# Hybrid decoder trunk on one core: another bank pool for the second half of the last gate, and a fixed place for the block transposes

## The chip, the core and the metric

The kernel runs on one core of one Trainium2 chip (TRN2). The metric is the device time of one execution in microseconds (us), and the time of a kernel is the median of its runs. The engines are named as in the profile: PE is TensorE (PEld its weight loads), DVE is VectorE, ACT is ScalarE, POOL is GpSimd, SP is SyncE, which here only issues DMAs.

## The reference

One layer over 512 tokens of width 1024 in float32: a norm, one input projection shared by three token mixers with their own SiLU gates, an output projection with residual, a per-layer embedding that is let in by a sigmoid gate, and a last norm. The change lies in the last three steps.

```python
hn = rms_norm(h, norm_g[i])
z = hn @ w_in[i]
qa, ka, va, ga, xb, gb, uc, vc, gc = jnp.split(z, split_at, axis=-1)
ya = moba_attention(...) * jax.nn.silu(ga)
yb = multiscale_pool(xb, pool_w[i], pool_scale[i]) * jax.nn.silu(gb)
yc = spatial_gating(uc, vc, sgu_w[i], sgu_b[i]) * jax.nn.silu(gc)
h = h + jnp.concatenate([ya, yb, yc], axis=-1) @ w_out[i]
h = h + (p[i] @ ple_w[i]) * jax.nn.sigmoid(h @ ple_gate_w[i])
return rms_norm(h, final_g)
```

## The kernel before

**Numbers.** Every float32 product is made of three matmuls (`three`, L79 to L82): each operand is cut into a high part (a copy rounded by ACT) and a low part (the rest, by a DVE subtraction), and high times high, low times high and high times low are added in one PSUM bank. A tile of 128 x 512 results with a depth of 1024 is 24 matmuls of 512 columns.

**Weights.** All weights come as one stream of tiles of 128 x 1024 in a fixed order: the input projection, then eight tiles of `wo` (output projection, one for each 128 output channels), then eight of `wpg` (the gate's weights, here called G0 to G3 for output channels 0 to 511 and G4 to G7 for 512 to 1023). `fetch` issues a tile's DMA on SP's queue into one of three `raw` buffers. `cut` makes the high part on ACT (L129) and puts the subtraction for the low part (L117) on a list, `lows`; `flush` issues what is on the list. `hi` and `lo` have three buffers each. The last two tiles, G6 and G7, have places of their own (`last_ph`, `last_pl`). So a raw buffer comes free when DVE has made the low part out of it, and a buffer of `hi` when PE has done the matmuls that read it. The final gain `fg` is loaded last, into the raw buffer that G6 leaves.

**Banks.** PSUM has eight banks, in two pools of four: `pm` (projections, output projection) and `pa` (attention, the embedding's first half, the gate).

**The end of the program**, which is the part that the change touches:

1. Output projection, turns m = 0 to 7 (L732 to L749). The result of a turn is channels x tokens in a bank of `pm`. `residual` adds it to x on DVE (L727), cuts the sum into h_hi (ACT, L76) and h_lo (DVE, L77), and after each odd turn puts 16 block transposes on the list `blocks`, 64 in all. Each is one DVE instruction (L711) that turns a quarter strip of 32 x 32 blocks of h back to tokens x channels, into `h2`. `turn_back(6)` at the end of each turn from 2 on issues up to six of them.
2. Gate, first half (L772 to L780): for each of G0 to G3, 24 matmuls into four banks of `pa`, one for each 128 tokens; then `flush` and `turn_back` of an even share of the transposes that are left.
3. Gate, second half (L788 to L796, L817 to L839): `second(i, ...)` makes one 128-token tile at a time with G4 to G7, in a bank of `pa`. The last tile is made as two halves of 256 columns. Beside it runs the rest of the first half: `gated` is a sigmoid out of the bank (ACT, L758), a product with the embedding and a sum into `h2` (DVE, L760 and L761), and a square with a row sum (ACT, L764). The first sigmoid stands behind a load of ACT's table. POOL multiplies the final gain `fg` by a constant (L783) and, for the last tile, by h2 (L821).
4. `finish` and L840 to L857: the same for the second half, the last norm, and the output DMAs.

**Order.** The code is written in one order, and a scheduler then puts the instructions of each engine in a row of its own, which the engine works through in order. It may move an instruction ahead of others that were written earlier if the tiles allow it. `tc.issue_after(x)` forbids that: what is issued within it on the engine of x stands behind x.

Of the kernel before, what the change touches and what calls it, by code (L numbers as in the profile page):

```python
# [53 lines left out]
def trunk(ctx: ExitStack, tc: tile.TileContext, t: dict, out: bass.AP):  # L54
# [8 lines left out]
    pm = pool("pm", bufs=PM, space=bass.MemoryType.PSUM)  # L63
    pa = pool("pa", bufs=8 - PM, space=bass.MemoryType.PSUM)
# [4 lines left out]
    def bank(p, name):  # L69
        return p.tile([P, 512], F32, tag="mm" if p is pm else "at", name=name)  # L70
# [8 lines left out]
    def three(ps, lh, ll, rh, rl, first, last):  # L79
        return [lambda: nc.tensor.matmul(ps, lh, rh, start=first, stop=False),  # L80
                lambda: nc.tensor.matmul(ps, lh, rl, start=False, stop=False),  # L81
                lambda: nc.tensor.matmul(ps, ll, rh, start=False, stop=last)]  # L82

    def go(mms, n=UNIT):
        for i, m in enumerate(mms):
            m()
            if i % n == n - 1:
                yield
# [17 lines left out]
            nc.sync.dma_start(raw, stream[len(raws)])  # L106
            raws.append(raw)

    last_parts, lows, highs = [], [], []

    def flush():
        for z in lows:
            z()
        lows.clear()

    def low(hi, lo, raw):
# [16 lines left out]
    def take(n=1, ahead=3):  # L133
        j = used[0]
        used[0] += n
        flush()
        cut(max(j + n, j + ahead))
        if n > 1:
            flush()
        fetch(len(parts) + 3 - len(lows))  # L140
        return parts[j] if n == 1 else parts[j:j + n]
# [42 lines left out]
    for b, (lo_d, hi_d) in enumerate(bucket_ranges()):  # L184
        n = hi_d - lo_d + 1
        a = 511 - hi_d
# [40 lines left out]
    gain(1)  # L227
    cut(1)
    flush()
    for i in range(NT):  # L230
        with tc.issue_after(highs[0].ins) if i > 1 else nullcontext():
# [474 lines left out]
    blocks = []  # L706
# [4 lines left out]
        return lambda: nc.vector.transpose(dst, src)  # L711

    def turn_back(n):
        for z in blocks[:n]:
            z()
        del blocks[:n]

    h2h = big.tile([P, KD, S], F32R, tag="acth", name="h_hi")
# [14 lines left out]
    ps = [bank(pm, f"ps_h{m}") for m in range(2)]  # L733
# [9 lines left out]
    for m in range(2, KD):  # L743
        w = take()
        ps = bank(pm, f"ps_h{m}")
        part(m, ps, w, gates)
        flush()
        residual(m, ps)
        turn_back(OUT_BLOCKS)  # L749
# [22 lines left out]
    ps = [bank(pa, f"ps_g0{i}") for i in range(NT)]  # L772
    for c in range(4):
        wh, wl = take()
        for k in (2 * c, 2 * c + 1):
            z = slice((k % 2) * 512, (k % 2 + 1) * 512)
            for i in range(NT):
                run(three(ps[i], h2h[:, k, i * P:(i + 1) * P], h2l[:, k, i * P:(i + 1) * P], wh[:, z], wl[:, z], k == 0, k == KD - 1))
        flush()
        turn_back(-(-len(blocks) // (4 - c)))  # L780
# [5 lines left out]
        side.append(gated(i, 0, 512, ps[i], h2[:, i, :512], sq[:, 4 * i:4 * i + 1]))  # L786

    def second(i, a, b, n):  # L788
        ps = bank(pa, f"ps_g1{i}{n}")[:, :b - a]
        mms = []  # L790
        for k in range(KD):
            wh, wl = w[k // 2]
            z = slice((k % 2) * 512 + a, (k % 2) * 512 + b)
            mms += three(ps, h2h[:, k, i * P:(i + 1) * P], h2l[:, k, i * P:(i + 1) * P], wh[:, z], wl[:, z], k == 0, k == KD - 1)
        yield from go(mms)
        return ps  # L796
# [12 lines left out]
    def ticking(g):  # L809
        while True:  # L810
            try:
                next(g)
            except StopIteration as z:
                return z.value
            tick()

    for i in range(NT - 1):  # L817
        ps = ticking(second(i, 0, 512, 0))
        side.append(finish(i, ps))
    i = NT - 1  # L820
    nc.gpsimd.tensor_tensor(h2[:, i, :512], h2[:, i, :512], fg[:, :512], op=ALU.mult)  # L821
    a, b = h2[:, i, 512:768], h2[:, i, 768:]
    ps = ticking(second(i, 0, 256, 0))
    def first_half():
        g = temp("gate_last0")[:, :256]
# [11 lines left out]

    side.append(first_half())
    ps2 = ticking(second(i, 256, 512, 1))  # L839
    while side:  # L840
        tick()
# [66 lines left out]
```

## Time and profile before

| | us |
|---|---|
| median of 3 runs | 295.53 |
| lowest and highest | 295.29, 296.71 |
| the profiled execution's own time | 294.94 |
| its span, first to last instruction | 293.2 |
| PE busy | 282.3 (96%) |
| DVE busy | 233.3 (80%) |
| ACT busy | 174.5 (60%) |
| POOL busy | 33.8 (12%) |

The span is what the trace shows; 1.74 us of the profiled execution lie around it. The share of busy time is a mean over stages, so the end of the program is read by itself: the output projection's turns 2 to 7 take 206.88 to 239.51 us, the gate's first half 239.51 to 261.29, the second half 263.78 to 286.14, and the rest is the last tile's norm and output.

### The profile page before, as it was taken

The numbers are of one execution on the slowest core, as the hardware profiler recorded it, in microseconds if no ns is written. First come the engines' busy times: TensorE is split into PE (matmuls) and PEld (weight loads), VectorE is DVE, ScalarE is ACT, GpSimd is POOL, SyncE is SP. The second block draws the span as 40 slices with busy tenths as digits, with TensorE's granted clock in tenths as the row PEclk, the third lists the DMA queues.
The fourth block names the chain that finished last, engine by engine and source line by source line (L and its number), as shares of the span: only waits on it lengthen the run. The fifth ranks groups of instructions, "written<-read, shape, count | busy, mean of one in ns | idle before, by whom it ended". The sixth has DMA issues, their size and how long they took to land.

```text
span 293.2 us, 4190 instructions
## 1 busy us (share of the span) xinstructions
PE 282.3 (96%) x1402; PEld 236.8 (81%) x1402; DVE 233.3 (80%) x562; ACT 174.5 (60%) x357; POOL 33.8 (12%) x82
## 2 busy tenths in 40 slices
PE   8999999999999999999999999999999999969990
PEld 6878888788899888888888888888888888858890
DVE  3799999577977899888868868562899999968664
ACT  5994674667775756656699999650432332176231
POOL 6933050000002110000000000000000000005121
PEclk9999999999999999999999999999999999999997
DMA  6989343322312042222222222275242223250033
GB/s 208 387 262 360 100 162 109 131 72 74 102 43 74 5 139 74 74 72 74 72 72 72 75 73 72 74 210 220 80 133 75 73 72 92 77 191 0 3 143 143
DMA packets 12949, 33.26 MB, mean 113 GB/s; under 512 B 1912, under 2 KB 2680, under 8 KB 12928
## 3 DMA queue, kind: packets, MB, share of 16 engines
q1 hardware_dynamic: 12464, 32.47, 33.1%
q10 hardware_dynamic: 432, 0.52, 0.5%
q8 instruction: 11, 0.18, 0.3%
q14 instruction: 10, 0.08, 0.1%
q0 software_dynamic: 32, 0.00, 0.0%
HBM read 30.87 MB, written 2.12 MB: 113 GB/s over the span
## 4 chain that ended last, share of the span: by engine, by line
PE 65%; DVE 16%; ACT 9%; issue 4%; DMA 3%; POOL 1%; SPq 1%; POOLq 0%; DVEq 0%; ACTq 0%
PE ps_g L80 7%; PE ps_g L82 7%; PE ps_g L81 7%; PE ps_h L81 5%; PE ps_h L80 5%; PE ps_h L82 5%; DVE lo L117 3%; DVE h L711 3%; PE ps_v L81 3%; PE ps_v L82 2%; PE ps_v L80 2%; ACT heads_qk L399 2%; PE ps_t L468 2%; DMA x<-in_xT 2%; ACT hi L129 1%
## 5 line engine op out<-in xcount | busy, mean ns | idle before, releaser
L129 ACT ACTIVATE hi<-raw 128x1024 fp32r<-128x1024 f32 x40 | 42.0, 1053 | 26.0 <-PE ps_h L81 12.2
L117 DVE TENSOR_TENSOR lo<-raw,hi 128x1024 fp32r<-128x1024 f32 x40 | 48.7, 1219 | 4.5 <-ACT hi L129 4.1
L711 DVE STREAM_TRANSPOSE h<-h 32x256 f32<-32x256 f32 x64 | 27.9, 436 | 0.9
L82 PE MATMUL ps_g<-hn_hi,lo 128*128 128x512 f32 x64 | 25.6, 399 | 0.0
L81 PE MATMUL ps_g<-hn_lo,hi 128*128 128x512 f32 x64 | 25.3, 396 | 0.0
L80 PE MATMUL ps_g<-hn_hi,hi 128*128 128x512 f32 x64 | 25.3, 395 | 0.0
L80 PE MATMUL ps_g<-hi,h_hi 128*128 128x512 f32 (+1 forms) x52 | 19.5, 375 | 2.3 <-ACT gate L758 2.3
L81 PE MATMUL ps_g<-lo,h_hi 128*128 128x512 f32 (+1 forms) x52 | 19.4, 373 | 0.0
L82 PE MATMUL ps_g<-hi,h_lo 128*128 128x512 f32 (+1 forms) x52 | 19.4, 373 | 0.0
L76 ACT ACTIVATE h_hi<-h 128x512 fp32r<-128x512 f32 x8 | 4.9, 629 | 18.3 <-DVE h L727 18.3
L117 DVE TENSOR_TENSOR pl<-ps_t,ph 128x128 fp32r<-128x128 f32 (+3 forms) x32 | 15.5, 483 | 0.4
L471 ACT ACTIVATE ph<-ps_t 128x128 fp32r<-128x128 f32 (+3 forms) x32 | 13.7, 427 | 2.8 <-PE ps_t L468 2.4
L463 POOL MEMSET ph<- 128x128 f32 x8 | 1.9, 236 | 113.0 <-PE ps_o L484 73.9
L81 PEld LDWEIGHTS ps_g<-hn_lo,hi 128*128 128x128 f32 x64 | 12.0, 188 | 2.3
L468 PE MATMUL ps_t<-flip,s 128*128 128x128 f32 x80 | 13.9, 272 | 0.0
L82 PEld LDWEIGHTS ps_g<-hn_hi,lo 128*128 128x128 f32 x64 | 12.0, 188 | 2.2
L80 PEld LDWEIGHTS ps_g<-hn_hi,hi 128*128 128x128 f32 x64 | 12.0, 188 | 2.1
L80 PEld LDWEIGHTS ps_g<-hi,h_hi 128*128 128x128 f32 x52 | 9.8, 188 | 4.5 <-ACT gate L758 2.8
L449 ACT ACTIVATE s<-s,st 128x128 f32<-128x128 f32 (+1 forms) x16 | 7.2, 451 | 10.0 <-DVE st L439 9.8
L446 ACT ACTIVATE s<-s,st 128x128 f32<-128x128 f32 (+1 forms) x16 | 7.2, 452 | 9.9 <-DVE st L434 9.9
L468 PEld LDWEIGHTS ps_t<-flip,s 128*128 128x128 f32 x80 | 10.4, 140 | 3.0
L457 DVE TENSOR_SCALAR s<-s,st 128x128 f32<-128x128 f32 (+3 forms) x32 | 12.2, 384 | 0.7
(226 smaller groups left out, 856.2 us busy)
## 6 DMA issues: line engine op xcount, KB each, us to landing
raw<-in_wg SPq DMA_DIRECT2D x8, 512.0 KB, 3.3
raw<-in_wo SPq DMA_DIRECT2D x8, 512.0 KB, 3.3
raw<-in_wpg SPq DMA_DIRECT2D x8, 512.0 KB, 3.3
x<-in_xT SPq DMA_DIRECT2D x8, 256.0 KB, 5.5
raw<-in_wv SPq DMA_DIRECT2D x4, 512.0 KB, 6.2
bias<-tab_d SPq DMA_DIRECT2D x8, 256.0 KB, 5.4
raw<-in_wq SPq DMA_DIRECT2D x4, 512.0 KB, 5.1
raw<-in_wk SPq DMA_DIRECT2D x4, 512.0 KB, 3.5
```

The source lines that it names most:

```text
L80: return [lambda: nc.tensor.matmul(ps, lh, rh, start=first, stop=False), lambda: nc.tensor.matmul(ps, lh, rl, start=False, stop=False), la ...
L81: lambda: nc.tensor.matmul(ps, lh, rl, start=False, stop=False),
L82: lambda: nc.tensor.matmul(ps, ll, rh, start=False, stop=last)]
L117: return lambda: nc.vector.tensor_tensor(lo, raw, f(hi), op=ALU.subtract)
L129: highs.append(nc.scalar.activation(hi, raws[j], AF.Copy))
L399: nc.scalar.activation(kh[e][r[z]], ps[r[e]], AF.Copy)
L446: nc.scalar.activation(sc[:, :n], sc[:, :n], AF.Exp, bias=st[:, 0:1], scale=-1.0, accum_out=st[:, 1:2])
L449: nc.scalar.activation(sc[:, 256:n], sc[:, 256:n], AF.Exp, bias=st[:, 0:1], scale=-1.0, accum_out=st[:, 7:8])
L457: nc.vector.tensor_scalar(sc[:, :n], sc[:, :n], st[:, 2:3], None, op0=ALU.mult)
L468: nc.tensor.transpose(ps[:, j * P:(j + 1) * P], probs[h, i][:, j * P:(j + 1) * P], flip)
L471: nc.scalar.activation(ph[:, :n, iq], src, AF.Copy)
L711: return lambda: nc.vector.transpose(dst, src)
```

## The change

The edit has two parts.

First, `second` takes its bank from `pm` in place of `pa`. In the second half the four tiles of the first half stay in `pa` until their sigmoids have read them; the banks of `pm` held the output projection's turns.

Second, `flush` notes the last low part that it issued, and `turn_back` issues its transposes within `tc.issue_after` of that instruction, so that a share of transposes stands behind that low part in DVE's row.

```diff
-    last_parts, lows, highs = [], [], []
+    last_parts, lows, highs, done = [], [], [], [None]
 
     def flush():
         for z in lows:
-            z()
+            done[0] = z()
         lows.clear()
...
     def turn_back(n):
-        for z in blocks[:n]:
-            z()
+        with tc.issue_after(done[0].ins):
+            for z in blocks[:n]:
+                z()
         del blocks[:n]
...
     def second(i, a, b, n):
-        ps = bank(pa, f"ps_g1{i}{n}")[:, :b - a]
+        ps = bank(pm, f"ps_g1{i}{n}")[:, :b - a]
         mms = []
```

No instruction is added or taken away. The rows of ACT, POOL and SP are the same before and after but for line numbers; PE's matmuls stand in the same order, and DVE's differ in where the transposes stand.

DVE's row in turns 5 to 6 of the output projection, before (`ps_h_2463` is the bank of turn 5, `ps_h_2503` of turn 6; `lo_2499` is the low part of G0, `lo_2539` that of G1; `h_2214`, `h_2217` and `h_2220` hold the sums of turns 2 and 3, 4 and 5, 6 and 7, and `h_2223` is `h2`):

```order
L727 TENSOR_TENSOR h_2217<-ps_h_2463,h_2217 128x512
L117 TENSOR_TENSOR lo_2499<-raw_2421,hi_2498 128x1024
L77 TENSOR_TENSOR h_lo<-h_2217,h_hi 128x512
L711 STREAM_TRANSPOSE h_2223<-h_2217 32x2x4x32 x9
L727 TENSOR_TENSOR h_2220<-ps_h_2503,h_2220 128x512
```

And there after the change:

```order
L728 TENSOR_TENSOR h_2217<-ps_h_2463,h_2217 128x512
L117 TENSOR_TENSOR lo_2499<-raw_2421,hi_2498 128x1024
L77 TENSOR_TENSOR h_lo<-h_2217,h_hi 128x512
L711 STREAM_TRANSPOSE h_2223<-h_2214 32x2x4x32 x6
L728 TENSOR_TENSOR h_2220<-ps_h_2503,h_2220 128x512
```

Six transposes stand between two turns' sums where nine stood; three of them are left for later.

DVE's row during the gate's first half, before (`lo_2584` is the low part of G2, `lo_2621` of G3, `lo_2658` of G4, `lo_2695` of G5; `last_pl<-raw_2660` that of G6, `last_pl<-raw_2697` that of G7):

```order
L117 TENSOR_TENSOR lo_2584<-raw_2501,hi_2583 128x1024
L77 TENSOR_TENSOR h_lo<-h_2220,h_hi 128x512
L711 STREAM_TRANSPOSE h_2223<-h_2220 32x2x4x32 x12
L117 TENSOR_TENSOR lo_2621<-raw_2541,hi_2620 128x1024
L711 STREAM_TRANSPOSE h_2223<-h_2220 32x2x4x32 x3
L117 TENSOR_TENSOR lo_2658<-raw_2586,hi_2657 128x1024
L117 TENSOR_TENSOR last_pl<-raw_2660,last_ph 128x1024
L117 TENSOR_TENSOR lo_2695<-raw_2623,hi_2694 128x1024
L117 TENSOR_TENSOR last_pl<-raw_2697,last_ph 128x1024
```

And there after the change:

```order
L117 TENSOR_TENSOR lo_2584<-raw_2501,hi_2583 128x1024
L77 TENSOR_TENSOR h_lo<-h_2220,h_hi 128x512
L711 STREAM_TRANSPOSE h_2223<-h_2217 32x2x4x32 x7
L117 TENSOR_TENSOR lo_2621<-raw_2541,hi_2620 128x1024
L711 STREAM_TRANSPOSE h_2223<-h_2217 32x2x4x32 x5
L711 STREAM_TRANSPOSE h_2223<-h_2220 32x2x4x32 x2
L117 TENSOR_TENSOR lo_2658<-raw_2586,hi_2657 128x1024
L711 STREAM_TRANSPOSE h_2223<-h_2220 32x2x4x32 x7
L117 TENSOR_TENSOR last_pl<-raw_2660,last_ph 128x1024
L117 TENSOR_TENSOR lo_2695<-raw_2623,hi_2694 128x1024
L711 STREAM_TRANSPOSE h_2223<-h_2220 32x2x4x32 x7
L117 TENSOR_TENSOR last_pl<-raw_2697,last_ph 128x1024
```

Twelve and three transposes became four shares of seven, and one share now stands ahead of G6's low part and one ahead of G7's.

PE's row at the start of the second half, as a difference (`ps_g_2740` is the bank of the first tile, `ps_g_2789` of the second; `hi_2657` is the high part of G4, `hi_2694` of G5; what an instruction waits for stands in brackets):

```order
 L81 MATMUL ps_g_2740<-lo_2658,h_hi 128x512
 L82 MATMUL ps_g_2740<-hi_2657,h_lo 128x512
-L80 MATMUL ps_g_2740<-hi_2694,h_hi 128x512
+L80 MATMUL ps_g_2740<-hi_2694,h_hi 128x512 [waits Activation_49]
 L81 MATMUL ps_g_2740<-lo_2695,h_hi 128x512 [waits DVE_49]
 L82 MATMUL ps_g_2740<-hi_2694,h_lo 128x512
```

The first tile's matmuls with G5 (and, not shown, with G7) now wait for ACT by themselves, and the first matmuls of the second and later tiles no longer do, but for the very last half tile.

## Rows read from the trace of the kernel before

**Rows 1.** Busy time of each engine by stage, with granted clock (windows).

```profile
core 0: us, PE busy (x) PEld busy (x) DVE busy (x) ACT busy (x) POOL busy (x), PEclk, DMA share, GB/s
...
239.51:261.29 21.78, 21.78 (x97) 17.83 (x95) 19.49 (x33) 6.78 (x8) 0.00 (x0) 1.00 0.30 97
261.29:263.78 2.49, 0.15 (x2) 0.00 (x1) 1.50 (x3) 2.46 (x4) 0.00 (x0) 1.00 0.55 211
263.78:286.14 22.36, 22.36 (x120) 19.33 (x120) 15.84 (x25) 8.84 (x23) 6.85 (x6) 1.00 0.13 48
286.14:293.20 7.06, 0.00 (x1) 0.00 (x0) 3.00 (x10) 0.89 (x2) 0.66 (x1) 0.72 0.39 149
```

**Rows 2.** The chain that ended last: start, duration, engine, tile and line.

```profile
257.42 3.31 DMA raw<-in_wpg
260.76 1.06 ACT last_ph L129
261.83 1.28 ACT L758
263.13 0.61 ACT gate L758
```

**Rows 3.** PE's instructions in order of time; idle time and releaser in brackets.

```profile
233.86 0.39 PE L82 MATMUL ps_h<-y4ph,lo 128*128 128x512 f32 x1
...
261.06 0.39 PE L82 MATMUL ps_g<-hi,h_lo 128*128 128x512 f32 x1
...
263.78 0.50 PE L80 MATMUL ps_g<-hi,h_hi 128*128 128x512 f32 x1 [2.33 <-ACT gate L758]
...
264.12 0.40 PE L81 MATMUL ps_g<-lo,h_hi 128*128 128x512 f32 x1
...
280.23 0.28 PE L80 MATMUL ps_g<-hi,h_hi 128*128 128x256 f32 x1
```

**Rows 4.** DVE's instructions in order of time, from turn 4's sum on.

```profile
226.57 0.69 DVE L727 TENSOR_TENSOR h<-ps_h,h 128x512 f32<-128x512 f32 x1
227.18 1.22 DVE L117 TENSOR_TENSOR lo<-raw,hi 128x1024 fp32r<-128x1024 f32 x1
228.31 0.68 DVE L77 TENSOR_TENSOR h_lo<-h,h_hi 128x512 fp32r<-128x512 f32 x1
229.00 4.05 DVE L711 STREAM_TRANSPOSE h<-h 32x256 f32<-32x256 f32 x9
...
239.47 0.69 DVE L727 TENSOR_TENSOR h<-ps_h,h 128x512 f32<-128x512 f32 x1
...
248.12 5.38 DVE L711 STREAM_TRANSPOSE h<-h 32x256 f32<-32x256 f32 x12
253.53 1.23 DVE L117 TENSOR_TENSOR lo<-raw,hi 128x1024 fp32r<-128x1024 f32 x1
...
256.17 1.23 DVE L117 TENSOR_TENSOR lo<-raw,hi 128x1024 fp32r<-128x1024 f32 x1
...
261.85 1.23 DVE L117 TENSOR_TENSOR last_pl<-raw,last_ph 128x1024 fp32r<-128x1024 f32 x1 [0.30 <-ACT last_ph L129]
...
264.37 1.53 DVE L760 TENSOR_TENSOR gate<-gate,ple 128x512 f32<-128x512 f32 x1
```

**Rows 5.** ACT's instructions in order of time, in the gate.

```profile
250.65 1.06 ACT L129 ACTIVATE hi<-raw 128x1024 fp32r<-128x1024 f32 x1 [3.10 <-issue]
...
274.99 0.60 ACT L758 ACTIVATE gate<-ps_g 128x512 f32<-128x512 f32 x1 [1.12 <-PE ps_g L82]
...
280.43 0.60 ACT L758 ACTIVATE gate<-ps_g 128x512 f32<-128x512 f32 x1 [2.57 <-PE ps_g L82]
```

**Rows 6.** DMA issues from 205 us on: size, median us to landing.

```profile
raw<-in_wpg SPq DMA_DIRECT2D x8, 512.0 KB, 3.3
```

**Rows 7.** POOL's multiplication of the final gain, in order of time.

```profile
264.08 3.02 POOL L783 TENSOR_SCALAR fg<-fg 128x1024 f32<-128x1024 f32 x1 [82.77 <-DMA fg<-in_fg]
```

**Rows 8.** DVE's gate products: count, minimum, median and maximum duration in ns.

```profile
L760 DVE TENSOR_TENSOR gate<-gate,ple x7: 678/693/1526, 263.8 to 281.1; 128x512 f32<-128x512 f32 x7
```

## The prediction

> **What bounds the kernel now.** I read the stages first. Through the gate's first half, 239.51 to 261.29 us, PE is busy for all of its 21.78 us, and in the second half, 263.78 to 286.14, for all of its 22.36; between them lies a stretch of 2.49 us in which PE is busy 0.15 [rows 1]. So the end of the program is bound by PE but for that hole, and whatever closes it moves the end, as long as the work behind PE's last matmul, 7.06 us, only moves along [rows 1]. PE's row tells what the hole waits for: the last matmul of the first half starts at 261.06, the first of the second half at 263.78, and what released it is a sigmoid on ACT [rows 3]. The wait is for a bank: that sigmoid is the first that empties a bank of `pa`, and all four are full. The chain shows why it comes so late. ACT works in order, and the sigmoid stands behind the high part of G7 and a table load. G7's DMA is issued at 257.42, its high part runs from 260.76, the table load from 261.83, the sigmoid from 263.13 [rows 2]. G7's DMA waited in turn for a raw buffer, which DVE freed with the low part that it began at 256.17, behind twelve transposes from 248.12 and a low part at 253.53 [rows 4]. So the hole has two causes in a row: the bank, and a DVE queue in which transposes stand ahead of low parts. The change touches each.
>
> **Part one, the bank.** With a bank of `pm` the first matmul needs only G4 and a bank whose turn was summed up long ago: the last use of `pm` is turn 7's sum. The matmuls' pace is (280.23 - 264.12) / 71 = 0.227 us for 512 columns [rows 3]. The row after the last of the first half would thus start at 261.06 + 0.23 = 261.29, not 263.78: 2.49 us. The first step after the hole took 264.12 - 263.78 = 0.34 in place of 0.227 [rows 3], another 0.11. Then the 73rd matmul of the second half starts at 261.29 + 72 x 0.227 = 277.63, not 280.23: **2.60 us earlier**. From there on the row of PE is the same.
>
> That holds if each weight is there when PE comes to it. PE needs G4 at 261.29, G5 six matmuls later at 262.65, G6 at 264.0, and G7's low part at the 20th, 261.29 + 19 x 0.227 = 265.6. Before, G7's low part ended at 261.85 + 1.23 = 263.08 [rows 4], so part one alone would do it, with 2.5 us to spare.
>
> **Part two, the transposes.** Nothing is added on DVE: 64 transposes stay 64. A turn of the output projection cost DVE 0.69 for the sum, 1.22 for a low part, 0.68 for h_lo and 4.05 for nine transposes, 6.6 us [rows 4], against 24 x 0.227 = 5.44 on PE. So DVE fell behind: turn 6 ended on PE at 233.86 + 0.39 = 234.25, and its sum started at 239.47 [rows 3, 4], 5.2 us late. With six transposes (0.45 each) the turn costs 5.3, and DVE keeps up. Turn 7 ends on PE at 234.25 + 5.44 = 239.7, and its sum starts there. The shares of seven cost 3.15 each, and I lay them out with the same durations:
>
> - Low part of G2 240.4 to 241.6, h_lo to 242.3, seven transposes to 245.5.
> - G3's high part needs the buffer of G0, which PE leaves at 239.51 + 5.44 + 0.2 = 245.1; with 1.06 on ACT it is there at 246.2. Low part to 247.4, seven to 250.6.
> - G4's high part starts at 250.65 as before, since it waits for PE to leave G1 [rows 5]. Low part 251.7 to 252.9, seven to 256.1.
> - G6 takes G3's raw buffer: DMA from 247.4, 3.3 to landing [rows 6], high part behind G4's to 252.8. Low part 256.1 to 257.3.
> - G5's high part waits for PE to leave G2 at 255.9, to 257.1. Low part to 258.5, seven to 261.7.
> - G7's DMA lands at 252.9 + 3.3 = 256.2, its high part runs to 258.2, and its low part, behind the seven, 261.7 to **262.9**.
>
> The deadline is 265.6, so 2.7 us are left. The new wait is that of each share behind a low part; what queues behind a share is the next low part, and for each the sum above has it in time. So part two costs nothing and, with part one there, brings nothing that PE sees: the low parts of G3 and G4 come earlier than PE wants them. It does move G7's high part and the table load (1.28 [rows 2], 258.2 to 259.5) ahead of the first half's end, so the first sigmoid could run from 259.5 to 260.1, before PE wants its bank at 261.29. By this sum part two alone would close the hole as well; the gains of the two parts are one and the same 2.60 and don't add. SP's row is the same, its issues only come earlier, and the queue is far from full (0.30 of the DMA engines' time in the first half [rows 1]).
>
> **One collision.** POOL multiplies `fg` for 3.02 us, from 264.08 before [rows 7]. The gate product that DVE began at 264.37 took 1.53 us [rows 4], the median of the seven is 0.69 [rows 8]: 0.84 more. `fg` follows G6 into its buffer, so it now lands near 257.3 + 3.3 = 260.6, and POOL works into 263.6, over G7's low part, itself a product of two SBUF inputs. With 0.84 more the low part ends at 263.8, still 1.8 ahead of its deadline. The floor is no collision, 262.9; the ceiling is that DVE stands still until POOL is done, 263.6 + 1.2 = 264.9, still 0.7 ahead. I take 263.8, as the row is of the same kind. The Trainium skill, page "SBUF — State Buffer", section "Who interferes with whom", says that a VectorE instruction with two SBUF inputs contends with a GpSimd instruction that reads SBUF, and one with a single input does not. Its other rule, that the side which comes second stands still for the whole of the other's instruction, is stated for the two-port modes; taken here it would be the ceiling. The row speaks for the first and against the second, since 0.84 is not 3.02.
>
> **Behind PE.** The first half's products then start between 262.9 and 264.9, before at about 263.8. What hangs on them is ACT's sigmoid of each second-half tile. Before, ACT stood idle 1.12 us until PE finished the second tile and 2.57 until it finished the third [rows 5]. With PE 2.60 earlier, and the first-half work no earlier at all, the second tile's sigmoid is 1.12 earlier, held by ACT, and the third is PE's again with 1.12 + 2.57 - 2.60 = 1.09 to spare. So from the third tile on all moves by 2.60, unless DVE starts more than 1.09 later than before. The clock is granted at 1.00, that is 2.4 GHz, in the hole and on both sides of it [rows 1], so the hole costs and gives no clock.
>
> **The sum.** The profiled execution had a span of 293.2 and a time of 294.94. Less 2.60 that is 290.6 and 292.34. The median of the runs is 0.59 above it, 295.53; less 2.60 that is **292.9 us**, 0.9% less.
>
> **The rivals.**
>
> 1. *The wait moves back to DVE and ACT.* The first half's products collide with POOL, start as late as 264.9, and ACT gets to the third tile after PE. Against it stands the 1.09 us of slack, for it that POOL now meets DVE's queue at a fuller place. If POOL starts 0.4 later than I put it, the products start 1.5 later than before and 0.4 are lost; with a second collision of 0.84 it is 1.3. Time 293.3 to 294.2.
> 2. *The change doesn't do what it says*, no change, 295.5. Both ways out would have to fail: PE's first matmul of the second half still waits for a count of ACT that takes in the sigmoid, and the transposes don't bring G7 forward, so that the chain of [rows 2] holds. Against the first: in PE's new row the matmuls with G5 and G7 wait for ACT by themselves, which they would not need after a wait for the sigmoid. Against the second: the sum for DVE above.
> 3. *Slower: G7's low part is late.* It is now the last of a row of 28 held transposes. If DVE does not catch up and stays 5.2 us behind, as at turn 6 [rows 3, 4], the low part ends at 262.9 + 5.2 + 0.84 = 268.9, and PE stands 3.3 us at its 20th matmul: 292.9 + 3.3 = 296.2. The point from which it costs at all is an end after 265.6, and it is slower than before from 268.2. Against it: at six transposes the turn is shorter on DVE than on PE, by 0.1 only, and from turn 7's sum to the last share DVE's row holds 0.69 + 0.68 + 5 x 1.22 + 28 x 0.45 = 20.1 us of work for 22.0, the time from 239.7 to 261.7. That is little room, and the weakest step.
>
> **How the numbers follow.** Within 0.5% (1.48 us, about what a measurement can tell from no change) is 294.05 to 297.0. Forecast, 292.9: 0.84. Rival 1: 0.08, nearly all of it still faster. Rival 2: 0.04. Rival 3: 0.04, half of it within 0.5%. Faster 0.91, same 0.07, slower 0.02. For the range: the forecast's own uncertainty is the spread of medians, some 0.6 us, as between the profiled time and the median here, so 292.2; upwards it takes in rival 1, 294.2. Rivals 2 and 3 stay out, about 1 in 10.
>
> **What would show it.** In the trace after: no idle time of PE between the gate's halves, and PE's first 256-column matmul at about 277.6. Sums that start within half a us of PE's end of each turn. G7's low part done by 263 to 264, and no PE wait for it. POOL's `fg` near 260.6 to 261. The sigmoids from about 259.5, and the stretch from PE's last matmul to the end still 7.1. Wrong would be a PE wait at G5 or G7, a hole that is still there, or an end stretch longer than 7.1.

## The result, and the profile after

The changed kernel takes **292.38 us** (median of 6 runs, 292.12 to 292.61), beside 296.43 for the kernel before (6 runs, 295.29 to 296.71). The ratio is 0.9872, with a 95% interval of 0.9853 to 0.9892: faster by 1.3%. The forecast was 292.9, in a range of 292.2 to 294.2. The profiled execution took 292.33 us, with a span of 290.6; the sum had 292.34 and 290.6.

PE's instructions at the seam between the gate's halves, and its first matmul of 256 columns, after the change (each line has start, duration, engine, line of the kernel, operation, tiles and shape):

```profile
261.06 0.39 PE L82 MATMUL ps_g<-hi,h_lo 128*128 128x512 f32 x1
261.28 0.39 PE L80 MATMUL ps_g<-hi,h_hi 128*128 128x512 f32 x1
...
277.60 0.28 PE L80 MATMUL ps_g<-hi,h_hi 128*128 128x256 f32 x1
```

These answer to [rows 3]. The first half's last matmul starts at 261.06 in both traces, to the hundredth. Before, the next one started at 263.78; now it starts at 261.28, one step of PE later. The first matmul of 256 columns stands at 277.60 for 280.23: 2.63 us earlier, and 2.6 is what the span lost. The stages, as in [rows 1]:

```profile
core 0: us, PE busy (x) PEld busy (x) DVE busy (x) ACT busy (x) POOL busy (x), PEclk, DMA share, GB/s
239.51:261.28 21.77, 21.77 (x97) 18.02 (x96) 19.38 (x36) 9.65 (x11) 0.00 (x0) 1.00 0.28 97
261.28:283.51 22.23, 22.23 (x121) 19.22 (x119) 17.13 (x27) 8.03 (x22) 6.63 (x6) 1.00 0.13 48
283.51:290.60 7.09, 0.00 (x1) 0.00 (x0) 3.00 (x10) 0.89 (x2) 0.66 (x1) 0.87 0.39 148
```

PE is busy through both halves, and the stretch behind its last matmul is as long as before, 7.09 for 7.06. DVE, in order of time, from turn 6's sum on (compare [rows 4]):

```profile
234.63 0.69 DVE L728 TENSOR_TENSOR h<-ps_h,h 128x512 f32<-128x512 f32 x1
...
239.79 0.69 DVE L728 TENSOR_TENSOR h<-ps_h,h 128x512 f32<-128x512 f32 x1
...
258.55 3.15 DVE L711 STREAM_TRANSPOSE h<-h 32x256 f32<-32x256 f32 x7
261.73 1.77 DVE L117 TENSOR_TENSOR last_pl<-raw,last_ph 128x1024 fp32r<-128x1024 f32 x1
263.43 1.28 DVE L761 TENSOR_TENSOR gate<-gate,ple 128x512 f32<-128x512 f32 x2
```

Turn 6 is summed up 0.4 us after PE ends it, where it was 5.2 before. G7's low part runs from 261.73 to 263.50. ACT in order of time (compare [rows 2, 5]):

```profile
257.01 1.04 ACT L129 ACTIVATE last_ph<-raw 128x1024 fp32r<-128x1024 f32 x1
258.07 1.28 ACT L759 ACT_TABLE_LOAD   x1
259.44 2.64 ACT L759 ACTIVATE gate<-ps_g 128x512 f32<-128x512 f32 x4
...
272.59 0.58 ACT L759 ACTIVATE gate<-ps_g 128x512 f32<-128x512 f32 x1
...
277.80 0.60 ACT L759 ACTIVATE gate<-ps_g 128x512 f32<-128x512 f32 x1 [2.36 <-PE ps_g L82]
```

G7's high part, the table load and the sigmoids stand 3.7 us earlier than in [rows 2], and the first sigmoid begins 1.8 us ahead of the seam at 261.28. POOL's multiplication of the final gain (compare [rows 7]):

```profile
261.37 2.81 POOL L784 TENSOR_SCALAR fg<-fg 128x1024 f32<-128x1024 f32 x1 [80.06 <-DMA fg<-in_fg]
```

It lies over the whole of G7's low part.

One thing doesn't fit: the spans differ by 2.6 us, the medians by 4.05. The runs of the changed kernel lie within 0.5 us, those of the kernel before within 1.4, in two groups: 295.29 and 295.53, then 296.28 to 296.71. The experiments had to settle two questions: which part of the change does it, and where the rest of the gain comes from.

### The profile page after: what moved, and what is told of

The parts are those of the page before. It is cut to its first block, busy times and chain, and to the rows that moved or that the text cites. A ratio compares the mean times of both kernels' runs of the same rounds, so it can differ in the third digit from the quotient of the medians.

```text
span 290.6 us, 4190 instructions
## 1 busy us (share of the span) xinstructions
PE 281.8 (97%) x1402; PEld 236.7 (81%) x1402; DVE 233.0 (80%) x562; ACT 174.9 (60%) x357; POOL 34.1 (12%) x82
## 4 chain that ended last, share of the span: by engine, by line
PE 87%; ACT 4%; issue 2%; DVE 2%; DMA 2%; SPq 1%; POOL 0%; POOLq 0%; DVEq 0%; ACTq 0%
PE ps_g L82 9%; PE ps_g L81 9%; PE ps_g L80 9%; PE ps_h L82 5%; PE ps_h L81 5%; PE ps_h L80 5%; PE ps_t L468 3%; PE ps_v L81 3%; PE ps_v L82 3%; PE ps_v L80 2%; PE ps_q L81 2%; PE ps_q L82 2%; PE ps_k L80 2%; PE ps_k L82 2%; PE ps_q L80 2%
## 5 line engine op out<-in xcount | busy, mean ns | idle before, releaser
L81 PE MATMUL ps_v<-lo,hn_hi 128*128 128x512 f32 x32 | 12.6, 393 | 0.3 <-DVE lo L117 0.3
L80 PE MATMUL ps_v<-hi,hn_hi 128*128 128x512 f32 x32 | 12.7, 396 | 0.0
```

## Experiments

**The bank alone.**

```diff
-        ps = bank(pa, f"ps_g1{i}{n}")[:, :b - a]
+        ps = bank(pm, f"ps_g1{i}{n}")[:, :b - a]
```

> Part one alone: the second half's bank from pm, the transposes free to move as before. My theory (the two parts close the same hole): PE goes on at 261.3 us without a wait, G7's low part still ends at 263.1, ahead of the 265.6 at which PE wants it; the span is that of the full change, 290.6, and the time 292.4 (ratio to before as the full change, 0.987). The rival that each part closes a share of the hole: a time between, near 294. The rival that the bank is not what PE waits for: no change from before.

Measured: 292.26 us, ratio 0.9889 (0.9865 to 0.9913), against 295.04 for the kernel before beside it. PE at the seam, DVE and ACT of its trace, in which this part runs 0.2 us later as a whole:

```profile
261.23 0.39 PE L82 MATMUL ps_g<-hi,h_lo 128*128 128x512 f32 x1
261.46 0.39 PE L80 MATMUL ps_g<-hi,h_hi 128*128 128x512 f32 x1
```

```profile
261.97 1.23 DVE L117 TENSOR_TENSOR last_pl<-raw,last_ph 128x1024 fp32r<-128x1024 f32 x1 [0.30 <-ACT last_ph L129]
```

```profile
263.25 2.07 ACT L758 ACTIVATE gate<-ps_g 128x512 f32<-128x512 f32 x4
...
277.98 0.60 ACT L758 ACTIVATE gate<-ps_g 128x512 f32<-128x512 f32 x1 [1.24 <-PE ps_g L82]
```

The sigmoids are as late as before, 263.25, and PE has no wait at the seam: its next matmul starts 0.23 us after the last of the first half. The third tile's sigmoid still waits for PE, with 1.24 us to spare; the sum had 1.09 for this very case. The bank alone gives the whole gain.

**The held transposes alone.**

```diff
-            z()
+            done[0] = z()
...
-        for z in blocks[:n]:
-            z()
+        with tc.issue_after(done[0].ins):
+            for z in blocks[:n]:
+                z()
```

> Part two alone: transposes held behind the low parts, the second half's bank from pa as before. My theory: G7's high part and the table load come before the first half ends, the first sigmoid ends at 260.1, so the bank is free when PE wants it at 261.3; no hole, span 290.6, time 292.4. The rival that only the bank matters: the hole of 2.5 us stays and the time is that of before. The rival that each part closes a share: near 294.

Measured: 292.35 us, ratio 0.9895 (0.9872 to 0.9919); five of six executions took 292.0 to 292.4, one 293.1, and no trace shows why. ACT, then PE, of its trace, in which this part runs 0.3 us earlier as a whole:

```profile
259.14 2.64 ACT L759 ACTIVATE gate<-ps_g 128x512 f32<-128x512 f32 x4
```

```profile
260.75 0.39 PE L82 MATMUL ps_g<-hi,h_lo 128*128 128x512 f32 x1
260.98 0.39 PE L80 MATMUL ps_g<-hi,h_hi 128*128 128x512 f32 x1
```

PE's first matmul of the second half still depends on the first sigmoid, but that one starts at 259.14 and takes some 0.6 us, so the bank is free before PE gets to it at 260.98. So the hole had two causes in a row, either part removes one of them, and one is enough. The gains don't add.

**G7's low part late, by twelve, four and eight transposes.** These are the full change with repeats of transposes, which write the same values once more, between the last held share and G7's low part (here for twelve):

```diff
+    with tc.issue_after(done[0].ins):
+        for n in range(12):
+            again = block(3, n % 4, n // 4)()
...
-    w = take(4)
+    flush()
+    cut(used[0] + 4)
+    g7 = lows.pop()
+    flush()
+    with tc.issue_after(again.ins):
+        g7()
+    w = parts[used[0]:used[0] + 4]
```

> As the run with twelve, with four repeated transposes: 1.8 us. My theory: G7's low part ends by 264.8 to 265.3, still ahead of 265.6, the products start 1.3 to 1.8 us later, inside the 2.4 us that ACT stands idle before the third tile's sigmoid; no loss, span 290.6, time 292.4. The rival that DVE's delays reach the end one for one: 294.2.

> As the run with twelve repeated transposes, with eight. By the deadline theory G7's low part starts 3.6 us later than in the full change, at 265.3, ends at 266.5, and PE, which wants it at 265.6, stands 0.9 to 1.0 us; a hole of one us leaves the clock alone, so the end moves by 1.0 to 1.1: span 291.7, time 293.4, and all executions lie within a few tenths. The rival that any hole here brings the clock down: 294.7 in a part of the executions.

> The full change with twelve more transposes (repeats, they write the same values again) between the last held share and G7's low part. My theory of the deadline: the low part starts 12 x 0.45 = 5.4 us later, at 267.1, and without POOL beside it ends at 268.3; PE wants it at 265.6 to 265.8 and stands 2.5 to 2.8 us; the end moves by that and no more, span 293.2, time 295.0, about the kernel before. The rival that DVE's delays reach the end one for one: 290.6 + 5.4 = 296.0, time 297.8. The rival that the products and sigmoids behind are the tighter path: more than 2.8.

| repeats | median us | range | PE's wait for G7's low part, us |
|---|---|---|---|
| 0 (the change) | 292.38 | 292.12 to 292.61 | none |
| 4 | 292.27 | 292.24 to 292.70 | none |
| 8 | 293.39 | 293.21 to 293.94 | 0.93 |
| 12 | 296.72 | 295.16 to 297.32 | 2.51 |

With four, DVE begins the low part at 263.62 and the third tile's sigmoid has 2.58 us to spare; DVE, then ACT:

```profile
263.62 1.23 DVE L117 TENSOR_TENSOR last_pl<-raw,last_ph 128x1024 fp32r<-128x1024 f32 x1
```

```profile
277.80 0.60 ACT L759 ACTIVATE gate<-ps_g 128x512 f32<-128x512 f32 x1 [2.58 <-PE ps_g L82]
```

With eight, PE waits 0.93 at its 20th matmul and then steps on at its full pace, 267.42, 267.65. This trace runs 0.4 us later as a whole, so the deadline stands at 266.0 in it; the low part ends at 267.03. PE:

```profile
267.09 0.50 PE L81 MATMUL ps_g<-last_pl,h_hi 128*128 128x512 f32 x1 [0.93 <-DVE last_pl L117]
267.42 0.39 PE L82 MATMUL ps_g<-last_ph,h_lo 128*128 128x512 f32 x1
267.65 0.40 PE L80 MATMUL ps_g<-last_ph,h_hi 128*128 128x512 f32 x1
```

The deadline holds for these: four repeats cost nothing, and eight, 1.0 us past it, cost 1.0 in the median. The granted clock behind the wait is 1.00 (267.09 to 271.00). With twelve the wait is as long as expected, 2.51, but the trace's span is 294.5 and not 293.2. PE after the wait, and windows from the same trace:

```profile
267.97 0.50 PE L81 MATMUL ps_g<-last_pl,h_hi 128*128 128x512 f32 x1 [2.51 <-DVE last_pl L117]
268.31 0.46 PE L82 MATMUL ps_g<-last_ph,h_lo 128*128 128x512 f32 x1
268.57 0.63 PE L80 MATMUL ps_g<-last_ph,h_hi 128*128 128x512 f32 x1
268.99 0.63 PE L81 MATMUL ps_g<-last_pl,h_hi 128*128 128x512 f32 x1
```

```profile
267.97:271.95 3.98, 3.98 (x10) 3.13 (x11) 3.98 (x7) 1.82 (x5) 0.00 (x0) 0.57 0.00 0
271.95:276.00 4.05, 4.05 (x19) 3.34 (x18) 2.39 (x5) 2.06 (x6) 2.07 (x2) 1.00 0.00 0
```

Behind the hole the granted clock is 0.57 over 4 us (PEclk, the third number from the right), and from 268.57 to 271.95 the matmuls step by 0.40 to 0.43 us instead of 0.227: the clock stood at the lower of its two levels, 1.2 GHz. Ten matmuls took 3.98 where 0.34 for the step behind the wait and 9 x 0.227 would be 2.38: 1.6 us lost. It is not in every execution: 2 of the 10 took 295.2 with a mean clock of 0.996 and 0.997, which is the expected 295.0, and 8 took 296.2 to 297.3 with 0.985 to 0.991. Only one of the eight was traced; that the others lost their time in the same place is read from their times and clocks. So the theory of the deadline stands, and a second cost showed: a hole of 2.5 us can be followed by a fall of the clock. The Trainium skill, page "TensorE: Matmul & The Clock Gate", section "What's actually happening", says that a gate in front of the array passes full or half of the pulses by how busy the engine has lately been; the rows agree with the two levels and the direction. That raised the question whether the hole of the kernel before does the same.

**The kernel before, traced again.** No edit.

> The kernel before, unchanged, for a second trace of it. Its executions so far fall in two groups, 11 of 17 at 294.5 to 295.4 us with a mean granted clock of 0.993 to 0.995 and 6 at 296.2 to 297.1 with 0.988 to 0.990. My theory: in the second group TensorE's clock falls to 1.2 GHz for some 3 us after the hole between the gate's halves and costs 1.3 to 1.5 us; if this trace is of that group (some 4 in 10), the granted clock after 263.8 us is below 1 and the matmuls there step by 0.43 us instead of 0.227. If it is of the first group, the trace is as the one before. The rival (a DMA or a start that is late): the slow stretch lies elsewhere and the clock after the hole is 1.00.

This trace is one of the slower group (the upper group, below): 296.85 us, span 295.1, mean clock 0.988. PE at the seam, and windows; below them, for comparison, the same window of the first trace:

```profile
261.35 0.39 PE L82 MATMUL ps_g<-hi,h_lo 128*128 128x512 f32 x1
264.08 0.66 PE L80 MATMUL ps_g<-hi,h_hi 128*128 128x512 f32 x1 [2.35 <-ACT gate L758]
264.54 0.63 PE L81 MATMUL ps_g<-lo,h_hi 128*128 128x512 f32 x1
...
267.52 0.47 PE L82 MATMUL ps_g<-hi,h_lo 128*128 128x512 f32 x1
267.84 0.39 PE L80 MATMUL ps_g<-hi,h_hi 128*128 128x512 f32 x1
```

```profile
261.29:263.90 2.61, 0.45 (x2) 0.02 (x1) 1.90 (x2) 2.58 (x3) 0.00 (x0) 1.00 0.63 198
263.90:268.00 4.10, 3.92 (x10) 3.10 (x11) 3.94 (x6) 2.77 (x8) 3.21 (x1) 0.58 0.01 2
268.00:272.00 4.00, 4.00 (x19) 3.27 (x19) 1.81 (x4) 2.05 (x7) 1.23 (x2) 1.00 0.00 0
```

```profile
263.90:268.00 4.10, 4.10 (x19) 3.37 (x20) 4.10 (x6) 2.64 (x7) 3.02 (x1) 1.00 0.00 0
```

The hole is the same as in [rows 3], 2.35 against 2.33 us. But the eight steps from 264.08 to 267.52 took 0.43 each, 3.44 in all where 0.34 for the step behind the wait and 7 x 0.227 would be 1.93: 1.5 lost, at a granted clock of 0.58 over the window, and then 1.00 again. In the first trace the clock after the hole was 1.00. The spans of the two traces differ by 1.9: some 0.3 is there already when PE reaches the seam, and the rest, 1.6, arises in the ten matmuls behind it, so the rival of a late start holds for 0.3 of it only. The two groups, in the executions of the kernel before for which a mean clock is listed (those of the first row were measured on another chip than the rest):

| executions | lower group: number, clock, mean us | upper group: number, clock, mean us |
|---|---|---|
| beside the first four experiments | 11 of 17, 0.993 to 0.995, 294.92 | 6 of 17, 0.988 to 0.990, 296.46 |
| beside the last four | 9 of 23, 0.993 to 0.995, 295.00 | 14 of 23, 0.988 to 0.990, 296.34 |
| of this run itself | 5 of 8, 0.993 to 0.996, 294.89 | 3 of 8, 0.988, 296.40 |

**The hole filled.** The kernel before, with ten matmuls into a bank that nobody reads. PE's second half still depends on the sigmoid, but PE works meanwhile.

```diff
     w = take(4)
+    fill = bank(pm, "ps_fill")
+    for n in range(10):
+        nc.tensor.matmul(fill, h2h[:, 0, :P], w[0][0][:, :512], start=True, stop=True)
```

> The kernel before, with ten matmuls of 512 columns into a bank that nobody reads, between the gate's halves: 10 x 0.227 = 2.27 us of the 2.49 us hole is filled, the hole as a delay stays, since PE still waits for the sigmoid until 263.8. My theory (the hole costs twice, as a delay of 2.6 us in every execution and through the clock in some): all executions fall in the lower group of the kernel before, 294.5 to 295.4, none near 296.3, and the mean clock is 0.993 or more. The rival that the upper group has another cause: as many executions near 296.3 as before, 4 in 10.

Measured: 294.89 us, 12 runs from 294.37 to 295.25, mean clock 0.991 to 0.997; ratio to the kernel before 0.9968 (0.9953 to 0.9984). PE, and a window:

```profile
261.17 2.43 PE L787 MATMUL ps_fill<-hi,h_hi 128*128 128x512 f32 x10
263.70 0.50 PE L80 MATMUL ps_g<-hi,h_hi 128*128 128x512 f32 x1
```

```profile
263.90:268.00 4.10, 4.10 (x19) 3.35 (x19) 4.10 (x6) 2.56 (x7) 3.15 (x1) 1.00 0.00 0
```

The second half starts as late as before, 263.70, yet not one of 12 executions lies in the upper group, which held 14 of the 23 beside it; the lowest clock, 0.991, is below what the expectation named but goes with 294.6. Their mean, 294.88, is that of the lower group, 295.00. Ten useless matmuls bring the median down by 0.3%, by taking the upper group away. So the hole costs twice: 2.6 us as a delay in every execution, and 1.3 to 1.5 us through the clock in a part of them. That the whole upper group is such a fall of the clock rests on one trace of it, on the mean clocks, and on its absence here.

**The products late.** The full change with eight repeated transposes between G7's low part and the first gate product, so that PE's weights are in time and only what follows the sigmoids is late.

```diff
     w = take(4)
+    with tc.issue_after(done[0].ins):
+        for n in range(8):
+            again = block(3, n % 4, n // 4)()
+    late = [again]
...
-        nc.vector.tensor_tensor(g, g, ple[i][:, c0:c0 + n], op=ALU.mult)
+        with tc.issue_after(late[0].ins):
+            nc.vector.tensor_tensor(g, g, ple[i][:, c0:c0 + n], op=ALU.mult)
```

> The full change with eight repeated transposes between G7's low part and the first gate product on DVE: the products start 3.6 us later, at 267.0, PE's weights are in time. My theory (behind PE there is slack of 2.4 us at the third tile, where ACT stood idle 2.36 us in the trace of the change): PE waits for nothing, the third tile's sigmoid comes about 1.2 us late, and half to all of that reaches the end: span 291.1 to 291.8, time 292.9 to 293.5. The rival that only PE counts: 292.4. The rival that the delay reaches the end one for one: 296.

Measured: 292.03 us (2 runs), span 290.3: nothing lost. My theory missed, and the rival that only PE counts came true. DVE, then ACT:

```profile
266.77 1.29 DVE L762 TENSOR_TENSOR gate<-gate,ple 128x512 f32<-128x512 f32 x2
```

```profile
269.95 0.58 ACT L759 ACTIVATE gate<-ps_g 128x512 f32<-128x512 f32 x1
...
277.45 0.60 ACT L759 ACTIVATE gate<-ps_g 128x512 f32<-128x512 f32 x1 [0.87 <-PE ps_g L82]
```

The products start 3.34 us later than in the change, in a trace that runs 0.35 earlier as a whole, and the third tile's sigmoid still has 0.87 to spare, so 1.5 of the 2.36 were used and not 3.3. With the products late the scheduler put the second half's first sigmoid ahead of two of the first half's squares on ACT, at 269.95, only 0.9 later than in the change (269.06). So the path behind PE is looser than its idle time says, as the order follows the delay.

## Why the prediction was right, and what it missed

- **The bound and the hole.** Right. PE bounds the end, and the 2.49 us and the slower first step are gone: 2.63 measured for 2.60.
- **Part two.** Right, nearly row by row. DVE keeps up with the turns; the low parts of G3 and G4 begin at 246.30 and 251.74 (sum: 246.2 and 251.7), the last share at 258.55 (258.5), the sigmoids at 259.44 (259.5). The remark that part two alone would close the hole was shown by its own run, and so was that of part one.
- **The collision with POOL.** Right in kind, the size smaller, the time of it later. POOL began at 261.37, 0.8 later than the 260.6 of the sum. G7's low part took 1.77 us beside it in the change and 1.23 in the run with four repeats, where it started 2.1 us behind POOL instead of 0.4: 0.54 more, for 0.84 assumed. It ended at 263.50 instead of 263.8. The transposes beside POOL's 2.8 us in the run with twelve, 8.60 for 19 or 0.453 each, cost what they cost elsewhere. That agrees with the Trainium skill, page "SBUF — State Buffer", section "Who interferes with whom", on one and two SBUF inputs; that the side which comes second stands still for the whole instruction is not what happened here, since the low part was done 0.68 before POOL. Nor did every instruction with two SBUF inputs pay: the first gate product began at 263.43, while POOL was still listed as busy, and took its usual 0.68. What decides between them no run shows.
- **The slack behind PE.** The 1.09 us was right for the case that it was worked out for, products no earlier than before: 1.24 in the run with the bank alone. In the change itself the slack is 2.36, as the products start 0.33 earlier and the first sigmoid after them 1.18 earlier; the collision with POOL that one product had before now falls on G7's low part, ahead of them.
- **The clock: the step that was wrong.** "The hole costs and gives no clock" was read from a single trace, in which the clock stayed at 1.00 after the hole. That trace was of the lower group. The second trace of the same kernel shows 0.58 after the same hole. The sum of the time stayed right because it was made against the lower group: the bank alone is 2.66 us below that group (294.92 less 292.26, run beside it). That the trace at hand was of this group was luck. The same sum from the second trace, 296.85 less 2.60, would have been 294.25, 1.9 above the result. And the 0.59 that was added for the median does not show in the result: 292.34 without it, 292.38 measured. But the ratio came out at 0.987, where 292.9 of 295.53 is 0.991: the median of the kernel before, 296.43, lies in the upper group, and the change takes that group away. So the gain, 4.05 us between medians for 2.60 forecast, was undersized by what the clock costs. Three runs, of which one stood 1.2 above the other two, had hinted at it; I read them as scatter.
- **The rivals.** None came true. The condition of the first did, POOL 0.8 later than the sum had it, but not its price, as DVE didn't stand still until POOL was done: the products started at 263.43 and not behind 264.9. The third, a late low part of G7, was brought about by twelve repeats: with PE held up for 2.5 us it is slower than the kernel before, ratio 1.0033 (1.0010 to 1.0057), as that rival had it for 2.6 us past the deadline, but most of the difference goes with the clock; the two executions with the higher mean clock took 295.2.

What stays open: what decides, in one execution, whether the clock falls after a hole of this length. The traces show that it does or doesn't behind the same hole, not why.

## What to carry to other kernels

When an engine that bounds the end waits at a seam, follow the wait back through all its causes: here a full bank pool, and behind it an in-order queue in which work that nobody waited for (the transposes) stood ahead of the low part that freed a transfer's buffer. Removing any one link may be enough, so try each alone before adding up gains. And look at the spread of the runs before taking one trace for the kernel: two groups with two mean clocks are a sign that a hole in PE's row may cost more than its length, and filling the hole with work that nobody reads tests it.

## What the runs showed of the hardware

- A hole of 2.3 to 2.5 us in PE's row, with PE busy before and after it, was followed in some executions by a granted clock that stood at 1.2 GHz for the next eight matmuls or so (steps of 0.43 us), in others by full clock. By their times and mean clocks it was 23 of 48 executions of the kernel before, and 8 of 10 with twelve repeats; a trace shows it for one of each. With a hole of 0.93 us none of 4 executions was late by as much, and with the hole filled by matmuls none of 12.
- A mean granted clock of 0.988 against 0.994 over 293 us looks like nothing; within the kernel before it goes with 1.3 to 1.5 us. Between kernels it tells less: an execution with the bank alone had 0.991 and took 292.49.
- DVE transposes of 32 x 256 float32 run at 0.45 us each beside a POOL operation on SBUF, as without one; a DVE subtraction of two SBUF tiles that began 0.4 us after the same operation took 1.77 us for 1.23, and a product of two SBUF tiles that began 2.1 us after it the usual 0.68.
